# A hybrid decoder step: scaled tiles of the second norm tied to their splits, and four subtractions moved to GpSimd

## The chip, the cores and the metric

The kernel runs on one core of a Trainium2 chip. The metric is the device time of one execution in microseconds (us); the figure for a kernel is the median of its runs.

## What is computed

The reference is one decoder layer for 512 prompt tokens and 32 sample tokens (544 columns in all), with width 1024 and a feed-forward width of 2816. Only its end matters here:

```python
x = x + merged @ w_out
h2 = rmsnorm(x, norm2_g)
x = x + (silu(h2 @ w_ffn_gate) * (h2 @ w_ffn_up)) @ w_ffn_down
```

Ahead of it come the first norm, linear attention with a matrix state, dilated window attention, and the merge of both; behind it a last norm. Window caches of the sample tokens are also copied out.

## The kernel before

Activations lie transposed: 128 channels on the partitions, the 544 tokens along the free axis, cut into two halves of 272 columns (`cols`; index `i` or `hf_`, 0 or 1). A float32 number is carried as two parts, a high one that ScalarE makes by a copy into TensorE's rounded type and a low one, the difference, that VectorE makes (`split`, line 232: `act.activation` at L238, then `tt` at L230). Each product of matrices is three: high by high, low by high, high by low (`gemm`, line 327). Weights go through the same split (`wh`, `wlo`, two buffers each).

**The second norm.** For each half of the tokens the output projection is added to the residual `x2` (tiles `xres`), the squares are summed, `rates` makes the reciprocal root and `second` (line 1217) spreads it over the partitions by a small matmul into `zb`. Then eight scalar_tensor_tensor operations of VectorE (L1229, through the helper at L227) write the scaled tiles `hf{i}_{j}`, two for each of four tiles j, and four splits make `h2{i}h_{j}` and `h2{i}l_{j}`. For half 0 this happens within the projection of half 1. For half 1 `rates` and `second` are called in the middle of the matmuls of the first two feed-forward blocks on half 0 (`AT`, `mid`), so that TensorE has work while they run.

**The feed-forward.** Blocks 0 and 1 of gate (`fg`) and up (`fu`) run first on half 0 and then on half 1 (line 1252), block 0 into the wide PSUM tile `d`, of which there are two, block 1 into `zf`. Blocks 2 and 3 run plainly on both halves, each gemm into a `d`. `gated` takes them out: tanh on ScalarE (L1246), then two operations of VectorE on the tile `y`; a `d` is free when VectorE's operation has read it.

Blocks 4 to 21 go in pairs by a scheme of seven products (Strassen's, in Winograd's form) on 2 by 2 blocks: `mov` holds the seven operands made of tokens, `sta` those made of weights. Four of the token operands are sums of scaled tiles: `n5`, `n6`, `n4`, `n7`, each of two tiles of 128 x 544, made by `summed_up` (line 1288) on VectorE and split by `operand` (line 1276). Products 7 and 4 use `n7` and `n4`; the first of them comes some 26 us after the last low part. The weights' sums come by transfers: `fetch(0)` (line 1309) loads a block into `f0d` and `f0e` by SyncE's queue and adds a second block to them by two accumulating transfers that GpSimd issues (L1328, L1329). `prep_5` and `prep_7` then split `f0d` and `f0e` into `ws1` and `ws3`.

**What sets the order.** A planner orders each engine's instructions when the program is built, by its own estimates of when their inputs are ready; the engines then run their lists strictly in order. `pin` (`tc.keep_in_program_order`) ties an instruction behind the one that was written before it on its engine; it asks for order only, not for the end of that one. `nop` ties nothing. The two accumulating transfers in `fetch` are tied so, and so are the small copies `pace` on GpSimd (L298) and the transfers of window caches (L417) that follow a weight's split: `pace` reads a mark that the split's high part leaves, and thereby holds the next transfers of GpSimd's list back until that split is done.

```python
        nc.sync.dma_start(out=r2, in_=c2[:, 4:8])
        pin(pool.dma_start(out=s1, in_=c2[:, 4:8], accum_op=ALU.add))
        pin(pool.dma_start(out=s3, in_=c1[:, 0:4], accum_op=ALU.add))
```

In the program's text `fetch(0)` stands behind the last `operand` call, and on GpSimd nothing is written between the `pace` and cache copy of block 2's gate weights and these two transfers.

Of the kernel before, what the change touches and what calls it, by code (L numbers as in the profile page):

```python
# [5 lines left out]
F32 = mybir.dt.float32  # L6
# [3 lines left out]
AF = mybir.ActivationFunctionType  # L10
ALU = mybir.AluOpType
# [159 lines left out]
def build(tc, I, O, C):  # L171
    nc = tc.nc
    act, dve, pe, pool = nc.scalar, nc.vector, nc.tensor, nc.gpsimd
# [21 lines left out]
    def free(*tags):  # L195
        for t in tags:
            rings.pop(t)
# [18 lines left out]
    def dense_ps(ha=HA):  # L216
        t = psd.tile([P, 1024], F32, tag="d", name="d")
        return t[:, 512 - ha:512 - ha + NT]

    def mps(name="m", tag="m"):  # L220
        return psm.tile([P, 512], F32, tag=tag if SPLIT_PS else "m", name=name)

    def mm(out, lhsT, rhs, start=True, stop=True):
        return pe.matmul(out, lhsT=lhsT, rhs=rhs, start=start, stop=stop)  # L224

    def stt(out, in0, scalar, in1, op0, op1, **kw):
        return dve.scalar_tensor_tensor(out=out, in0=in0, scalar=scalar, in1=in1, op0=op0, op1=op1, **kw)  # L227

    def tt(out, a, b, op):
        return dve.tensor_tensor(out=out, in0=a, in1=b, op=op)  # L230

    def split(hi, lo, src, scale=1.0, pin=lambda i: i, later=None, **kw):
        def rest():
            if scale == 1.0:
                pin(tt(lo, src, hi.bitcast(F32), ALU.subtract))
            else:
                stt(lo, src, scale, hi.bitcast(F32), ALU.mult, ALU.subtract)
        pin(act.activation(out=hi, in_=src, func=AF.Copy, scale=scale, **kw))  # L238
        if later is None:
            rest()  # L240
        else:
            later.append(rest)

    def rsqrt(tp, x, n, tag, pin=lambda i: i):
        y = tp.tile([P, n], F32, name=tag + "i", tag=tag + "i")[:x.shape[0]]
        pin(pool.tensor_tensor(out=y, in0=x, in1=mhalf[0:x.shape[0], 0:n], op=ALU.pow))
        return y
# [54 lines left out]
    def dropped(keep):  # L302
        free(*[f"{keep}{n}{u}" for n in "hl" for u in range(2)])

    def weights(i, ahead=2, pin=lambda i: i, later=None):
        while state["next"] <= min(i + ahead, len(wl) - 1):
            emit_w(state["next"], pin, later)
            state["next"] += 1
        return ready[i]
# [12 lines left out]
    pin = tc.keep_in_program_order  # L322
# [4 lines left out]
    def gemm(i, xh, xl, halves=(0, 1), z=None, k0=0, first=True, last=True, ahead=2, cols=cols, fix=False, part=0, mid=None):  # L327
        _, _, nk, _, m, _ = wl[i]
        wide, m = m // P, min(m, P)
        wh, wlo = weights(i, ahead)  # L330
        if z is None:
            z = dense_ps()
        for k in range(nk):
            if mid and k == mid[0]:
                mid[1]()
            for j, (w, x) in enumerate(((wh, xh), (wh, xl), (wlo, xh))):
                for hf in halves:
                    (pin if fix else nop)(mm(z[hf] if type(z) is list else z[0:m, cols[hf][0]:cols[hf][1]], w(k * wide + part if wide > 1 else k), x(k0 + k, hf),
                       start=(first and k == 0 and j == 0), stop=(last and k == nk - 1 and j == 2)))
        due()  # L340
        return z
# [4 lines left out]
    def halved(ts):  # L346
        return lambda k, hf: ts[hf][k]
# [60 lines left out]
    for g in (2, 1, 0):  # L408
        step = (WIN[g] - 4) // (4 if g == 2 else 1)
        for nm in ("k", "v"):  # L410
            for b in range(8):
                for r0 in range(0, WIN[g] - 4, step):
                    src = I[f"state_win{g}_{nm}"][0, b, 4 + r0:4 + r0 + step].rearrange("r h d -> (r h d)").rearrange("(a n) -> a n", a=4)
# [14 lines left out]
    def late(t, ap, eng=None):  # L428
        tc.keep_in_program_order((eng or nc.gpsimd).dma_start(out=t, in_=ap))  # L429
        return t  # L430
# [4 lines left out]
    def vec_tile(name, ap, n):  # L435
        t = cst.tile([P, n], F32, name=name)
        nc.gpsimd.dma_start(out=t, in_=ap.rearrange("(k p) -> p k", p=P))
        return t

    def many(n, w, dt, name):  # L440
        return [one.tile([P, w], dt, name=f"{name}_{i}") for i in range(n)]
# [24 lines left out]
    for i in (0, 2, 1, 4, 3):  # L466
        n = x_src[i][1]
        j = junk[i % 2]
# [22 lines left out]
    zb = dense_ps(256)  # L491
# [677 lines left out]
    for m in range(8):  # L1169
        proj_a(m)  # L1170
        if m + AHEAD < 8:
            gate_a(m + AHEAD)
            if m + AHEAD == 7:
                free(*[f"{a}_{k}" for a in ("hh", "hl") for k in range(KD)])
                x2 = [late(t, xT_d[:, k]) for k, t in enumerate(many(KD, NT, F32, "xres"))]
# [3 lines left out]
    n2g = vec_tile("n2g", I["norm2_g"][0], 8)  # L1179
    h2h, h2l, hf = [], [], []  # L1180
    for i, (a_, b_) in enumerate(cols):
        n = b_ - a_
        acc = two.tile([P, HA], F32, tag="acc", name="acc")
        for m in range(8):
            z = [mps("zw")[:, 0:n]] * 2 if m % 2 else dense_ps()
            gemm(W["wo", m], halved(mgh), halved(mgl), halves=(i,), z=z, ahead=2 if i == 0 else W["fu", 0] - W["wo", m])
            z = z[i] if m % 2 else z[:, a_:b_]
            if i == 1:
                dropped(f"wo{m}")
                if m == FW:  # L1190
                    weights(W["fu", 1], 0, pin)
            tt(x2[m][:, a_:b_], x2[m][:, a_:b_], z, ALU.add)
            if m == 0:
                act.activation(out=acc[:, 0:n], in_=x2[m][:, a_:b_], func=AF.Square)
            else:
                sq = two.tile([P, HA], F32, tag="sq", name="sq")
                act.activation(out=sq[:, 0:n], in_=x2[m][:, a_:b_], func=AF.Square)
                tt(acc[:, 0:n], acc[:, 0:n], sq[:, 0:n], ALU.add)

        tiles = [(c, min(c + P, n)) for c in range(0, n, P)]  # L1200
        dgs = []

        def rates(i=i, acc=acc, tiles=tiles, dgs=dgs):
            zc = mps("zc")
            rt = two.tile([P, 3], F32, tag="rt", name="rt")
            dve.memset(rt, 1.0)
            for u, (c0, c1) in enumerate(tiles):
                (pin if i else nop)(mm(zc[0:c1 - c0, u:u + 1], acc[:, c0:c1], ones[:, 0:1]))
            for u, (c0, c1) in enumerate(tiles):
                dve.tensor_scalar(out=rt[0:c1 - c0, u:u + 1], in0=zc[0:c1 - c0, u:u + 1], scalar1=1.0 / D, scalar2=EPS, op0=ALU.mult, op1=ALU.add)  # L1210
            y = rsqrt(two, rt, 3, "r2")
            for u, (c0, c1) in enumerate(tiles):
                w_ = c1 - c0
                dgs.append(two.tile([P, P], F32, tag="dg2", name="dgt", bufs=3))
                dve.tensor_scalar(out=dgs[u][0:w_, 0:w_], in0=ident[0:w_, 0:w_], scalar1=y[0:w_, u:u + 1], scalar2=None, op0=ALU.mult)

        def second(i=i, a_=a_, b_=b_, n=n, tiles=tiles, dgs=dgs):
            zb = mps("zb")
            for (c0, c1), dgt in zip(tiles, dgs):
                w_ = c1 - c0  # L1220
                (pin if i else nop)(mm(zb[:, c0:c1], ones[0:w_, :], dgt[0:w_, 0:w_]))
            hi, lo = ([one.tile([P, 2, n], F32R, name=f"h2{i}{w}_{j}") for j in range(4)] for w in "hl")
            hf.append([one.tile([P, 2, n], F32, name=f"hf{i}_{j}") for j in range(4)])
            h2h.append([hi[k // 2][:, k % 2] for k in range(KD)])
            h2l.append([lo[k // 2][:, k % 2] for k in range(KD)])
            for j in range(4):
                for u in range(2):
                    m = 2 * j + u
                    stt(hf[i][j][:, u], x2[m][:, a_:b_], n2g[:, m:m + 1], zb[:, 0:n], ALU.mult, ALU.mult)  # L1229
                split(hi[j], lo[j], hf[i][j])  # L1230
            free(*[f"mg{i}_{m}" for m in range(8)])
            if i:
                free("acc", "sq", "rt", "r2i", "dg2")

        if i == 0:
            rates()
            second()
# [35 lines left out]
    def parts_of(h, l):  # L1273
        return [lambda k, t=t: t[k // 2][:, k % 2] for t in (h, l)]

    def operand(nm, src):
        hi, lo = ([one.tile([P, 2, HA], F32R, name=f"{nm}{w}_{j}") for j in range(2)] for w in "hl")
        for j in range(2):
            split(hi[j], lo[j], src[j])
        return parts_of(hi, lo)  # L1280

    def by_halves(i, k0):
# [5 lines left out]
    def summed_up(nm, f):  # L1288
        ts_ = [two.tile([P, 2, HA], F32, tag="nf", name=nm, bufs=4) for _ in range(2)]
        for j in range(2):  # L1290
            f(j, ts_[j])
        return ts_
# [5 lines left out]
    n4 = summed_up("n4", lambda j, t: stt(t, n6[j], -1.0, B21[j], ALU.mult, ALU.subtract))  # L1298
    mov[4] = operand("n4", n4)
    n7 = summed_up("n7", lambda j, t: tt(t, B22[j], B12[j], ALU.subtract))  # L1300
# [297 lines left out]
```

## Time and profile before

| what | us |
|---|---|
| median of 3 runs (lowest to highest) | 1061.74 (1059.97 to 1063.48) |
| the profiled execution, its own time | 1065.11 |
| its span in the trace | 1063.3 |
| TensorE (PE) busy | 1037.5 (98%) |
| VectorE (DVE) busy | 662.8 (62%) |
| ScalarE (ACT) busy | 458.6 (43%) |
| GpSimd (POOL) busy | 315.8 (30%) |

PE is TensorE's matmuls, PEld its weight loads. Times of rows count from the start of the span. A row of a timeline gives the start, the length, the engine, the line, the operation, the tile written and the tiles read, the shapes and the count, and in brackets how long the engine was idle before it and what it waited for. Neighbouring records overlap at their ends, since a next instruction enters the pipeline before the last has left it.

### The profile page before, as it was taken

To read this page: it belongs to the slowest core of one execution; us is meant where nothing else is said; L and a number is where in the kernel's file an instruction comes from. 1 tells how busy PE (TensorE), PEld (TensorE's weight loads), DVE (VectorE), ACT (ScalarE), POOL (GpSimd) and SP (SyncE) were. 2 spreads that over 40 slices of the span, in tenths; PEclk is the share of its full clock that TensorE was granted. 3 is DMA by queue.
4 is the path that set the end of the run, shared out by engine and by line. 5 is a ranking of instruction groups with operands and counts; after the bars stand their busy time and mean duration, and the time that the engine had idled before them with its cause. 6 is when DMAs were issued, how large, how long until landed. Compare 5 with 4: busy or idle time off the path is not lost.

```text
span 1063.3 us, 20293 instructions
## 1 busy us (share of the span) xinstructions
PE 1037.5 (98%) x7935; PEld 1001.0 (94%) x7935; DVE 662.8 (62%) x1232; ACT 458.6 (43%) x1016; POOL 315.8 (30%) x503
## 2 busy tenths in 40 slices
PE   6999999999999999999999999999999999999996
PEld 5999899899998999989989999999999999999996
DVE  5587665495686665636626566575988888933232
ACT  5454344663555543342323343353445454622222
POOL 2444232243453402222211211133343333122221
PEclk8999999999999999999999999999999999999998
DMA  8589537565586825536433554369999999443342
GB/s 236 139 223 259 164 96 203 152 201 171 162 267 193 284 65 171 177 114 199 145 98 119 164 159 129 100 186 225 281 261 275 274 298 250 153 151 102 113 114 84
DMA packets 207103, 190.30 MB, mean 179 GB/s; under 512 B 11120, under 2 KB 192080, under 8 KB 205728
## 3 DMA queue, kind: packets, MB, share of 16 engines
q0 software_dynamic: 35280, 95.63, 30.7%
q1 hardware_dynamic: 165440, 89.08, 30.2%
q10 hardware_dynamic: 6288, 4.29, 1.4%
q8 instruction: 62, 1.02, 0.4%
q14 instruction: 33, 0.27, 0.1%
HBM read 177.14 MB, written 55.67 MB: 219 GB/s over the span
## 4 chain that ended last, share of the span: by engine, by line
PE 90%; DMA 3%; DVE 3%; ACT 2%; issue 1%; POOL 0%; POOLq 0%; SPq 0%; DVEq 0%; ACTq 0%
PE d L224 61%; PE zs L224 9%; PE zo L224 5%; PE zB L224 3%; PE zw L224 2%; PE zl L224 2%; PE zA L224 1%; PE zu L224 1%; DMA raw<-in_w_out 1%; DMA f0e<-in_w_ffn_gate 1%; PE zq L224 1%; DMA x<-in_x_prompt 1%; PE zA L692 1%; DVE al L227 1%; PE zp L224 1%
## 5 line engine op out<-in xcount | busy, mean ns | idle before, releaser
L298 POOL COPY pace<-mark 1x1 f32<-1x1 f32 x109 | 82.1, 753 | 435.5 <-ACT wh L238 383.7
L224 PE MATMUL d<-hh,wh 128*128 128x272 f32 (+1 forms) x928 | 204.5, 298 | 4.2 <-ACT hh L238 2.2
L224 PE MATMUL d<-hl,wh 128*128 128x272 f32 (+1 forms) x928 | 202.6, 296 | 0.2 <-DVE hl L230 0.2
L238 ACT ACTIVATE wh<-raw 128x1024 fp32r<-128x1024 f32 (+1 forms) x97 | 100.3, 1034 | 232.4 <-PE d L224 152.7
L224 PE MATMUL d<-hh,wlo 128*128 128x272 f32 x912 | 196.6, 294 | 0.0
L230 DVE TENSOR_TENSOR wlo<-raw,wh 128x1024 fp32r<-128x1024 f32 (+1 forms) x96 | 115.4, 1202 | 101.1 <-ACT wh L238 100.8
L224 PEld LDWEIGHTS d<-hh,wh 128*128 128x128 f32 (+1 forms) x928 | 149.2, 190 | 7.7 <-ACT hh L238 2.3
L224 PEld LDWEIGHTS d<-hl,wh 128*128 128x128 f32 (+1 forms) x928 | 148.9, 190 | 4.0 <-issue 2.7
L224 PEld LDWEIGHTS d<-hh,wlo 128*128 128x128 f32 x912 | 146.1, 192 | 0.6
L224 PE MATMUL d<-al,wh 128*128 128x272 f32 x308 | 64.4, 291 | 2.0 <-DVE al L227 2.0
L224 PE MATMUL d<-ah,wh 128*128 128x272 f32 x308 | 64.9, 292 | 0.0
L224 PE MATMUL d<-ah,wlo 128*128 128x272 f32 x308 | 64.2, 290 | 0.0
L230 DVE TENSOR_TENSOR qb<-kt,qb 128x512 f32<-128x512 f32 x48 | 33.0, 688 | 44.7 <-DMA qb<-qd_d 44.4
L224 PEld LDWEIGHTS d<-al,wh 128*128 128x128 f32 x308 | 48.8, 190 | 2.5 <-DVE al L227 2.5
L224 PEld LDWEIGHTS d<-ah,wh 128*128 128x128 f32 x308 | 48.9, 191 | 0.1
L224 PEld LDWEIGHTS d<-ah,wlo 128*128 128x128 f32 x308 | 48.8, 190 | 0.0
L429 POOL DMA_DIRECT2D kt<-in_state_win_k x48 | 32.9, 685 | 12.2 <-DVE qb L230 7.5
L230 DVE TENSOR_TENSOR vl<-vt,vh 128x512 fp32r<-128x512 f32 (+1 forms) x40 | 25.0, 635 | 16.3 <-ACT vh L238 16.0
L238 ACT ACTIVATE vh<-vt 128x512 fp32r<-128x512 f32 (+1 forms) x40 | 23.0, 586 | 28.0 <-DMA vt<-in_state_win_v 17.3
L230 DVE TENSOR_TENSOR w12l<-raw,w12h 128x1024 fp32r<-128x1024 f32 x17 | 20.8, 1224 | 20.2 <-ACT w12h L238 20.2
L561 DVE TENSOR_REDUCE sall<-qb 128x8 f32<-128x512 f32 x48 | 32.7, 682 | 0.8
L429 POOL DMA_DIRECT2D vt<-in_state_win_v x40 | 21.7, 545 | 35.5 <-DVE vl L230 31.9
(562 smaller groups left out, 2831.8 us busy)
## 6 DMA issues: line engine op xcount, KB each, us to landing
raw<-in_w_in SPq DMA_DIRECT2D x58, 512.0 KB, 6.1
out_win_k_sample<-in_state_win_k POOLq DMA_DIRECT2D x32, 511.0 KB, 4.8
out_win_v_sample<-in_state_win_v POOLq DMA_DIRECT2D x32, 511.0 KB, 7.8
qb<-qd_d POOLq DMA_DIRECT2D x48, 256.0 KB, 5.1
kt<-in_state_win_k POOLq DMA_DIRECT2D x32, 256.0 KB, 5.3
vt<-in_state_win_v POOLq DMA_DIRECT2D x32, 256.0 KB, 4.3
raw<-in_w_ffn_down SPq DMA_DIRECT2D x16, 512.0 KB, 4.6
raw<-in_w_ffn_up SPq DMA_DIRECT2D x13, 512.0 KB, 6.3
```

The costliest lines, as they stand in the source:

```text
L224: return pe.matmul(out, lhsT=lhsT, rhs=rhs, start=start, stop=stop)
L227: return dve.scalar_tensor_tensor(out=out, in0=in0, scalar=scalar, in1=in1, op0=op0, op1=op1, **kw)
L230: return dve.tensor_tensor(out=out, in0=a, in1=b, op=op)
L238: pin(act.activation(out=hi, in_=src, func=AF.Copy, scale=scale, **kw))
L298: tc.keep_in_program_order(pool.tensor_copy(out=pace, in_=mark[0:1]))
L429: tc.keep_in_program_order((eng or nc.gpsimd).dma_start(out=t, in_=ap))
L561: dve.tensor_reduce(out=sall[:, g, 16 * b_:16 * b_ + 16].rearrange("p (t h) -> p t h", h=4)[:, :, 2 * hp:2 * hp + 2], in_=qb.rearrange("p ...
L692: pe.transpose(zA[:, v * P:(v + 1) * P], s[:, v * P:(v + 1) * P], ident)
```

## The change

In `second`, for half 1 alone, the scaled tiles and both parts of each split are tied in the order of the program's text, and that order is new: tiles 0, tiles 1, split 0, tiles 2, split 1, tiles 3, split 2, split 3. For half 0 the text's order is the same new one, but nothing is tied. In `operand` the splits are written out: the high part stays on ScalarE, the low part goes to GpSimd for `n4` and `n7` (two subtractions each) and stays on VectorE for `n5` and `n6`.

```diff
         def second(i=i, a_=a_, b_=b_, n=n, tiles=tiles, dgs=dgs):
             zb = mps("zb")
+            keep = pin if i else nop
             for (c0, c1), dgt in zip(tiles, dgs):
                 w_ = c1 - c0
                 (pin if i else nop)(mm(zb[:, c0:c1], ones[0:w_, :], dgt[0:w_, 0:w_]))
...
             for j in range(4):
                 for u in range(2):
                     m = 2 * j + u
-                    stt(hf[i][j][:, u], x2[m][:, a_:b_], n2g[:, m:m + 1], zb[:, 0:n], ALU.mult, ALU.mult)
-                split(hi[j], lo[j], hf[i][j])
+                    keep(stt(hf[i][j][:, u], x2[m][:, a_:b_], n2g[:, m:m + 1], zb[:, 0:n], ALU.mult, ALU.mult))
+                if j:
+                    split(hi[j - 1], lo[j - 1], hf[i][j - 1], pin=keep)
+            split(hi[3], lo[3], hf[i][3], pin=keep)
...
     def operand(nm, src):
         hi, lo = ([one.tile([P, 2, HA], F32R, name=f"{nm}{w}_{j}") for j in range(2)] for w in "hl")
         for j in range(2):
-            split(hi[j], lo[j], src[j])
+            act.activation(out=hi[j], in_=src[j], func=AF.Copy)
+            (pool if nm in ("n4", "n7") else dve).tensor_tensor(out=lo[j], in0=src[j], in1=hi[j].bitcast(F32), op=ALU.subtract)
         return parts_of(hi, lo)
```

## Rows read from the trace of the kernel before

**Rows 1.** Windows: PE, PEld, DVE, ACT, POOL busy us, clock, DMA share, GB/s.

```profile
680.00:700.00 20.00, 18.99 (x149) 18.62 (x149) 18.78 (x32) 11.34 (x20) 5.57 (x5) 1.00 0.16 54
700.00:720.00 20.00, 19.37 (x155) 19.19 (x154) 12.49 (x19) 7.19 (x14) 4.57 (x9) 1.00 0.80 232
720.00:740.00 20.00, 19.38 (x153) 19.01 (x152) 8.95 (x13) 6.38 (x13) 7.40 (x7) 1.00 0.97 215
740.00:800.00 60.00, 60.00 (x480) 60.00 (x479) 52.94 (x78) 29.90 (x53) 23.19 (x30) 1.00 1.08 264
```

**Rows 2.** Timeline of PE, the rows at its waits.

```profile
684.95 0.29 PE L224 MATMUL zf<-h21h,fu1h 128*128 128x272 f32 x1
686.25 0.39 PE L224 MATMUL d<-h21l,wh 128*128 128x272 f32 x1 [1.01 <-DVE h21l L230]
...
710.69 0.37 PE L224 MATMUL d<-h20h,wh 128*128 128x272 f32 x1 [0.63 <-DVE y L227]
...
739.02 0.40 PE L224 MATMUL d<-n6h,w24l 128*128 128x272 f32 x1 [0.62 <-DVE w24l L230]
```

**Rows 3.** Timeline of DVE.

```profile
681.58 3.35 DVE L227 SCALAR_TENSOR_TENSOR hf<-xres,n2g,zb 128x272 f32<-128x272 f32 x8
...
685.48 0.72 DVE L230 TENSOR_TENSOR h21l<-hf,h21h 128x544 fp32r<-128x544 f32 x1
...
695.86 0.72 DVE L230 TENSOR_TENSOR n<-hf,hf 128x544 f32<-128x544 f32 x1
...
701.75 0.72 DVE L230 TENSOR_TENSOR n7l<-n,n7h 128x544 fp32r<-128x544 f32 x1
...
707.64 0.69 DVE L230 TENSOR_TENSOR ws3l<-f0e,ws3h 128x512 fp32r<-128x512 f32 x1 [2.80 <-ACT ws3h L238]
...
709.83 0.71 DVE L227 SCALAR_TENSOR_TENSOR y<-y,d 128x544 f32<-128x544 f32 x1
```

**Rows 4.** Timeline of ACT.

```profile
682.51 0.66 ACT L238 ACTIVATE h21h<-hf 128x544 fp32r<-128x544 f32 x1 [1.32 <-DVE hf L227]
...
698.19 0.65 ACT L238 ACTIVATE n7h<-n 128x544 fp32r<-128x544 f32 x1
703.48 0.63 ACT L238 ACTIVATE ws1h<-f0d 128x512 fp32r<-128x512 f32 x1 [4.64 <-DMA f0d<-in_w_ffn_gate]
706.98 0.63 ACT L238 ACTIVATE ws3h<-f0e 128x512 fp32r<-128x512 f32 x1 [2.86 <-DMA f0e<-in_w_ffn_gate]
707.52 1.04 ACT L238 ACTIVATE wh<-raw 128x1024 fp32r<-128x1024 f32 x1
...
708.56 0.60 ACT L1246 ACTIVATE y<-d 128x544 f32<-128x544 f32 x1
```

**Rows 5.** Chain that ended last: start, length, what.

```profile
697.13 0.81 POOL f0d L1328
697.94 9.01 DMA f0e<-in_w_ffn_gate
...
710.69 12.23 PE d L224 x96
```

**Rows 6.** Timeline of POOL.

```profile
694.43 2.19 POOL L298 COPY pace<-mark 1x1 f32<-1x1 f32 x1 [18.22 <-ACT wh L238]
696.57 0.56 POOL L417 DMA_DIRECT2D out_win_v_sample<-in_state_win_v  x1
697.13 1.39 POOL L1328 DMA_DIRECT2D f0d<-in_w_ffn_gate  x1
697.94 1.90 POOL L1329 DMA_DIRECT2D f0e<-in_w_ffn_gate  x1
```

**Rows 7.** Groups of POOL instructions by shape, whole span: busy us, mean ns.

```profile
L933 POOL COPY qd<-q 128x512 f32<-128x512 f32 x4 | 2.5, 626 | 7.8 <-PE zs L224 7.8
```

**Rows 8.** Instructions that read the tile mark, ns min/median/max.

```profile
L298 POOL COPY pace<-mark x109: 173/892/2659, 16.6 to 1038.1; 1x1 f32<-1x1 f32 x109
```

**Rows 9.** Instructions that read the tile n7l, first and last start.

```profile
L224 PE MATMUL zs<-n7l,ws3h x72: 287/289/293, 728.9 to 910.6; 128*128 128x272 f32 x72
```

## The prediction

> **What bounds the kernel now.** I read the windows first. TensorE fills its stretches: around the change it is idle for 1.01 us in 680 to 700, 0.63 in 700 to 720 and 0.62 in 720 to 740, and not at all in the 60 us that follow, at a granted clock of 1.00 [rows 1]. So VectorE's work counts only where TensorE waits for it, and the three idle stretches, 2.26 us or 0.2% of the span, are all that this stage can give. The timeline of TensorE then shows one wait in each [rows 2]. At 685.24 it has done the four matmuls that want only the high part of the new half and stands until 686.25 for the first low part, `h21l`. At 710.06 it stands 0.63 us for VectorE to read a `d` that it wants for block 3. At 739.02 it waits for a weight's low part.
>
> The second wait is the one to look at, because the chain of waits runs through it. Behind `d` stands `y<-y,d` at 709.83 [rows 3], ahead of which ScalarE did, in this order, `ws1h`, `ws3h`, a weight's `wh` and the tanh of `y` [rows 4]. ScalarE stood until 706.98 for `f0e` to land, and only then came to the tanh, although the product that the tanh reads had long been there: 96 matmuls of this kind take 12.23 us [rows 5], so a gemm of 48 takes 6.1, and with TensorE running dry at 710.06 block 2's gate product ended near 704.0. The chain goes back through 9.01 us of the transfer into `f0e` to GpSimd, which issued `f0d` and `f0e` at 697.13 and 697.94 [rows 5, 6]. The end of the kernel thus hangs, at this place, on when GpSimd issues two transfers.
>
> **The tied order.** Nothing is removed: eight scaled tiles, four high parts, four low parts as before. VectorE runs the eight scaled tiles in 3.35 us, 0.41 apart, from 681.58, and the first low part starts at 685.48 after another operation that the planner put between [rows 3]; its high part was ready at 682.51 + 0.66 = 683.17 [rows 4]. Tied, the first low part comes fifth: 681.58 + 4 x 0.41 = 683.22, done at 683.94. TensorE wants it at 685.24, so the wait of 1.01 us goes, with 1.3 us to spare; one operation of 0.72 put between is covered too. Late next are the other high parts, since scaled tiles now wait behind low parts, each 0.64 from start to start (0.72 with the overlap): tiles 2 come 0.64 later than before, tiles 3 1.28, so the last high part ends near 686.9 and its low part near 687.6. TensorE needs 24 matmuls, about 3.0 us, for each tile j if it goes through all four products with it, and then has cover to spare; if the planner lets it run one product through all tiles, it wants tiles 3 some 2.25 us after 684.6, at 686.85, and stands up to 0.8 us. Gain 0.2 to 1.01; I take 1.01, because work of three other products lies ready.
>
> **The four subtractions.** Four operations of 0.72 us leave VectorE [rows 3]. It was busy 18.78 of 20 us there [rows 1], but no TensorE wait hangs on its load behind 686, so this is worth nothing by itself. On GpSimd nobody needs their results soon: the first matmul that reads `n7l` starts at 728.9 [rows 9], which hides them by far.
>
> What counts is GpSimd's list. The two accumulating transfers are tied behind what is written before them on GpSimd, which was a cache transfer and is now the last `n7l`. That one needs the last `n7h`, which ScalarE ends at 698.19 + 0.65 = 698.84 [rows 4], already past 697.13. The trace has no subtraction of this size on GpSimd. From below: a copy of 128 x 512 takes 626 ns [rows 7], for 544 columns 0.67 us. From above: a GpSimd copy of one element took 2.19 us at 694.43, against a shortest of 0.17 and a median of 0.89 [rows 8]; it ended within 0.05 us of a VectorE operation with two SBUF inputs, the one at 695.86 [rows 3, 6], as if held off by VectorE. I take twice the copy, 1.33 us, for two inputs read one after the other. [...]
>
> Starting when the cache transfer is issued, four subtractions last from 697.13 to 697.13 + 4 x 1.33 = 702.45, so `f0d` and `f0e` are issued 5.3 us later; with 0.67 they last to 699.8 (2.7 later), with 2.19 to 705.9 (8.8 later). What precedes may come up to 1.0 earlier with TensorE, so 4.3 net, between 1.7 and 8.8. Queued behind the transfers on GpSimd are `pace` copies and cache transfers, for which nobody in this stage waits; SyncE's loads go by their own queue.
>
> **Where that goes** depends on the planner's order on ScalarE. (a) If `ws1h` and `ws3h` stay ahead of `wh` and the tanh, the chain moves one for one with `f0e`, and the 1.01 gained above is eaten, since TensorE only arrives earlier at the same wait. (b) If the planner sees `f0e` land after 704.0, it puts `wh` and the tanh first. With both `ws` behind them the second wait vanishes too: -1.01 - 0.63 = -1.64. With only `ws3h` behind: `f0d` lands at 702.45 - 1.0 + (703.48 - 697.13) = 707.8, and by the spacing of the rows (0.54 to the next, 1.04, 1.27, 0.86 to TensorE) TensorE goes on at 711.5 instead of 710.69: +0.8. The planner had `f0e` landing before 704 by its own reckoning, else the order would not be what it is; a delay of several microseconds probably takes it past that.
>
> **Forecast**: (b), the middle of -1.64 and +0.8, -0.4 us. Against the profiled execution's 1065.11 that is 1064.7; the median of the runs lies 3.4 below the profiled one, so 1061.74 - 0.4 = 1061.3. Chance 0.5; alone its range is 1060.1 to 1062.6.
>
> **Rivals.**
> Order kept, (a): TensorE waits for `f0e` at block 3. +4.3, so 1066.0 (1.7 to 8.8: 1063.4 to 1070.5). For it: in the order of before both splits stood ahead, and ScalarE already stood for them. Against it: `f0e` took 9.01 us and `f0d` 6.35 with other loads beside them, and a later issue may find the queues emptier, which gives back up to 2.7. It decides, against my forecast, once `n7l` ends over 1 us after 697.13, and it passes the bound of 0.3% (3.2 us, about what a measurement of this kernel can tell from no change) where the net delay is over 3.2. Chance 0.35, two thirds of it beyond that bound.
>
> The tie does nothing: the wait at 686.25 becomes one of 0.8 for the later tiles, or the gain is waited away at 710, with `f0e` as late as before. Then 1061.5 to 1061.9. For it speaks that TensorE's order is planned anew. Chance 0.1.
>
> VectorE held by GpSimd: subtractions that keep VectorE out for their whole length take 4 x 1.33 = 5.3 us from it (8.8 at the upper bound), and 2.9 have been taken off its list. It ended its work on this stage at 701.75 + 0.72 = 702.47 [rows 3] and the `d` for block 2's second product is wanted near 704.0, so it has 1.5 us in hand; it costs from there, at most 8.8 - 2.9 - 1.5 = +4.4, 1066.1, and nothing at 1.33 (5.3 - 2.9 - 1.5 = 0.9). [...] Chance 0.05, of which half slower.
>
> **How the numbers follow.** Slower by over 0.3%: two thirds of 0.35 and half of 0.05, 0.26. Faster by over 0.3% would take 3.2 us where the idle of the stage is 2.26, so it needs an order changed elsewhere or a lucky median: 0.08. The rest is 0.66. The range goes from (b)'s lower end of 1060.1, less 0.3 for the spread of a median whose runs lay 1.75 apart to either side, 1059.8, to 1066.4, a little past the value of the kept order, leaving out its upper third.
>
> **What would show it.** Right: the first `h21l` starts near 683.2 and TensorE's gap of 1.01 us is gone; `f0d` is issued 2 to 6 us later behind four GpSimd subtractions of 0.7 to 2.2 us; on ScalarE `wh` and the tanh stand ahead of `ws3h`; TensorE's wait before block 3 is under 2 us. Wrong: `ws3h` still ahead of the tanh and a wait of 4 us or more at block 3; or the two transfers planned early after all, with the subtractions already done; or a low part that now waits for its high part and holds the scaled tiles behind it.

## The result, and the profile after

| kernel | median us (lowest to highest) | runs |
|---|---|---|
| before | 1062.17 (1059.97 to 1066.27) | 6 |
| changed | 1068.15 (1066.07 to 1071.02) | 6 |

The ratio is 1.0053, with a 95% interval of 1.0036 to 1.0070: 5.6 us slower (3.8 to 7.4). The forecast was 1061.3 and its range ended at 1066.4. The profiled execution took 1069.32 us, its span 1067.5.

The windows of the changed kernel answer to [rows 1]; the short one comes from narrower windows of the same view.

```profile
680.00:700.00 20.00, 17.38 (x137) 17.02 (x136) 17.56 (x28) 11.54 (x20) 6.36 (x3) 1.00 0.05 13
700.00:720.00 20.00, 17.50 (x126) 17.35 (x127) 12.73 (x16) 5.26 (x12) 10.58 (x15) 0.91 0.67 171
720.00:740.00 20.00, 20.00 (x162) 20.00 (x161) 6.50 (x10) 4.68 (x9) 7.41 (x7) 1.00 1.02 246
740.00:800.00 60.00, 59.57 (x474) 59.35 (x473) 53.07 (x78) 30.10 (x53) 22.21 (x26) 1.00 1.08 276
...
703.00:705.00 2.00, 2.00 (x11) 2.00 (x10) 2.00 (x3) 0.00 (x0) 2.00 (x4) 0.50 0.05 20
```

TensorE was idle for 2.26 us in these 120 us before [rows 1]; now it is idle for 5.55, and a stretch behind 702 also runs at a granted clock of 0.50 (703 to 705 above). TensorE's timeline says at which matmuls it stood (answers to [rows 2]).

```profile
700.86 0.37 PE L224 MATMUL d<-h20h,wh 128*128 128x272 f32 x1 [3.48 <-DVE y L227]
...
703.30 0.43 PE L224 MATMUL d<-h21l,wh 128*128 128x272 f32 x1
703.52 0.43 PE L224 MATMUL d<-h20h,wlo 128*128 128x272 f32 x1
...
716.28 0.37 PE L224 MATMUL d<-h20h,wh 128*128 128x272 f32 x1 [1.64 <-DVE y L227]
```

The wait of 1.01 us for `h21l` is gone, as forecast. In its place TensorE stands 3.48 us before block 2, for VectorE to read the `d` of block 0's gate product, and 1.64 us before block 3, where it stood 0.63. The matmuls from 702.20 to 705.56 start 0.226 us apart where they otherwise start 0.125 apart: 15 x 0.10 = 1.5 us more. The sum is -1.01 - 0.63 - 0.19 (from 0.62 to 0.43 at the weight's low part, at 739 before and near 744 now) + 3.48 + 1.64 + 1.5 = +4.8, within the measured interval.

Two traces do not start alike: the matmuls into `zb` of half 0, ahead of all that is tied, start at 654.16 before and at 654.76 in the changed kernel, so 0.6 us of every later difference between the two traces lies ahead of the stage (over all traces of this study that start lies between 650.1 and 654.8). From there to `zb` of half 1 both take 26.43 us, so the new order of half 0 costs nothing; from there to the first matmul that reads `n7l` (728.9 before, 734.5 now) the changed kernel takes 5.0 us longer, near the 4.8.

The chain shows what led to the 3.48. Two rows of before's chain first, not shown so far, then the changed kernel's.

```profile
691.18 1.90 PE d L224 x15
...
693.14 0.70 ACT wh L238
```

```profile
688.86 1.51 PE d L224 x12
690.37 1.50 PE zf L224 x12
...
695.47 0.57 ACT wh L238
...
698.26 1.82 DVE w22l L230
```

In the changed kernel TensorE goes through blocks 0 and 1 tile by tile, twelve matmuls into `d` and twelve into `zf` in turn. Before, it ran the last 15 matmuls that the chain follows into `d` in one piece and left `zf` for the end. So block 0's gate product is there 2.3 us later (695.47 against 693.14 at the `wh` that ScalarE does behind it; 1.7 without the shift of 0.6), and TensorE has used up the work that lay ready. Why the tiles come so late is seen on VectorE (answers to [rows 3]), the last low part of the kernel before first:

```profile
689.01 0.72 DVE L230 TENSOR_TENSOR h21l<-hf,h21h 128x544 fp32r<-128x544 f32 x1
```

```profile
684.44 0.72 DVE L230 TENSOR_TENSOR h21l<-hf,h21h 128x544 fp32r<-128x544 f32 x1
...
689.61 0.71 DVE L230 TENSOR_TENSOR h21l<-hf,h21h 128x544 fp32r<-128x544 f32 x1
690.24 0.71 DVE L1283 TENSOR_TENSOR n5l<-n,n5h 128x544 fp32r<-128x544 f32 x1
...
691.51 0.71 DVE L230 TENSOR_TENSOR h21l<-hf,h21h 128x544 fp32r<-128x544 f32 x1
...
696.65 1.69 DVE L230 TENSOR_TENSOR wlo<-raw,wh 128x1024 fp32r<-128x1024 f32 x1 [0.62 <-ACT wh L238]
698.26 1.82 DVE L230 TENSOR_TENSOR w22l<-f0c,w22h 128x512 fp32r<-128x512 f32 x1
700.01 0.71 DVE L227 SCALAR_TENSOR_TENSOR y<-y,d 128x544 f32<-128x544 f32 x1
```

Among the tied instructions the planner put token sums and their low parts, so the last `h21l` ends at 692.2, 10.1 us behind the first scaled tile at 682.17; before, it ended at 689.7, 8.2 us behind the one at 681.58. TensorE never stands for it here, since its order reads it first at 694.72. Ahead of the read of `d` stand `wlo` and `w22l`, which take 1.69 and 1.82 us; in the kernel before the same two took 1.22 and 0.68. GpSimd's list (answers to [rows 6]) has the subtractions where the forecast had them:

```profile
693.64 5.90 POOL L1283 TENSOR_TENSOR n4l<-n,n4h 128x544 fp32r<-128x544 f32 x2 [16.82 <-ACT n4h L1282]
...
700.68 2.66 POOL L1283 TENSOR_TENSOR n7l<-n,n7h 128x544 fp32r<-128x544 f32 x2
703.28 1.38 POOL L1332 DMA_DIRECT2D f0d<-in_w_ffn_gate  x1
704.12 1.86 POOL L1333 DMA_DIRECT2D f0e<-in_w_ffn_gate  x1
```

Both transfers are issued 6.2 us later than in [rows 6] (5.6 without the shift), and ScalarE keeps the order of [rows 4]: it waits for `f0d` and `f0e`, and only then does `wh` and the tanh that free block 3's `d`.

```profile
710.29 0.63 ACT L238 ACTIVATE ws1h<-f0d 128x512 fp32r<-128x512 f32 x1 [10.74 <-DMA f0d<-in_w_ffn_gate]
712.57 0.63 ACT L238 ACTIVATE ws3h<-f0e 128x512 fp32r<-128x512 f32 x1 [1.65 <-DMA f0e<-in_w_ffn_gate]
713.11 1.05 ACT L238 ACTIVATE wh<-raw 128x1024 fp32r<-128x1024 f32 x1
...
714.15 0.60 ACT L1249 ACTIVATE y<-d 128x544 f32<-128x544 f32 x1
```

### The profile page after: what moved, and what is told of

Read it like the earlier page. It is cut to its first block, busy times and chain, and to the rows that moved or that the text cites. A ratio compares the mean times of both kernels' runs of the same rounds, so it can differ in the third digit from the quotient of the medians.

```text
span 1067.5 us, 20294 instructions
## 1 busy us (share of the span) xinstructions
PE 1037.8 (97%) x7935; PEld 1001.2 (94%) x7935; DVE 664.2 (62%) x1228; ACT 459.0 (43%) x1016; POOL 325.9 (31%) x507
## 5 line engine op out<-in xcount | busy, mean ns | idle before, releaser
L230 DVE TENSOR_TENSOR wlo<-raw,wh 128x1024 fp32r<-128x1024 f32 (+1 forms) x96 | 118.5, 1235 | 103.3 <-ACT wh L238 102.8
```

## The experiments

All but the last two in one table, each against runs of the kernel before that were taken with it (medians 1061.41 to 1063.88); the times in us are the ratio and its interval times 1062. Idle is TensorE's in 680 to 800 of the profiled execution, the clock the granted one in 680 to 700 and in 700 to 720.

| kernel | ratio to before | us to before | idle us | clock |
|---|---|---|---|---|
| before | | | 2.26 | 1.00, 1.00 |
| changed | 1.0053 | +5.6 (3.8 to 7.4) | 5.55 | 1.00, 0.91 |
| the tie alone | 1.0011 | +1.2 (-0.4 to 2.7) | 2.79 | 0.91, 1.00 |
| the subtractions alone | 1.0001 | +0.1 (-1.3 to 1.6) | 1.80 | 1.00, 1.00 |
| changed, transfers early | 1.0062 | +6.6 (4.7 to 8.5) | 8.23 | 0.88, 0.86 |
| before, transfers early | 0.9995 | -0.5 (-1.8 to 0.7) | 1.03 | 1.00, 1.00 |
| the tie, sums late | 1.0030 | +3.2 (1.3 to 5.0) | 3.85 | 1.00, 0.91 |
| changed, subtractions behind the transfers | 1.0021 | +2.2 (0.6 to 3.8) | 2.47 | 0.93, 0.98 |
| the tie, sums late, transfers early | 0.9988 | -1.3 (-2.9 to 0.3) | 1.13 | 1.00, 1.00 |
| changed, `w22` late | 1.0012 | +1.3 (-0.2 to 2.8) | 3.76 | 1.00, 1.00 |
| changed, whole products | 1.0036 | +3.8 (2.1 to 5.5) | 4.63 | 0.83, 1.00 |
| sums late, transfers early, with the subtractions | 1.0007 | +0.7 (-0.8 to 2.3) | 1.85 | 1.00, 1.00 |

**The two halves apart.** The first kernel has only the part of the diff in `second`, the second only the part in `operand`.

> Only the tie; all eight low parts stay on VectorE. Theory A (the tie itself costs: with the low parts early, TensorE's list takes the four products of blocks 0 and 1 side by side, so block 0's gate product ends some 2.3 us later and its d is read too late for block 2): the 1.01 us wait is gone, a wait of 2 to 3 us stands before block 2, one of 0.5 to 1.5 before block 3; 1 to 3 us slower than before. Theory B (all of the loss comes from GpSimd: its subtractions hold VectorE and the two transfers): no wait before block 2, 1.0 us faster than before.

> Only the four subtractions on GpSimd; the second norm as before. Theory A: the 1.01 us wait stays, no wait before block 2, since block 0's gate product ends early as before; f0d is issued 4 to 7 us later; before block 3 a wait of 1 to 3 us; 0.5 to 2 us slower than before. Theory B: 4 to 6 us slower than before, most of it before block 3 or through VectorE operations stretched to 1.5 to 4 us.

With the tie alone the 1.01 us go and a wait before block 2 comes; the one before block 3 is gone.

```profile
696.18 0.47 PE L224 MATMUL d<-h20h,wh 128*128 128x272 f32 x1 [2.45 <-DVE y L227]
...
698.48 0.43 PE L224 MATMUL d<-h20h,wlo 128*128 128x272 f32 x1
698.71 0.43 PE L224 MATMUL d<-h21h,wlo 128*128 128x272 f32 x1
```

Behind the wait TensorE again runs 15 matmuls at 0.23 us from start to start, +1.5. The tie gives back all that it gained and perhaps a little more. The subtractions alone come out at nothing. Three engines of that kernel, GpSimd, VectorE, ScalarE:

```profile
694.14 2.69 POOL L1280 TENSOR_TENSOR n4l<-n,n4h 128x544 fp32r<-128x544 f32 x2
696.79 2.66 POOL L1280 TENSOR_TENSOR n7l<-n,n7h 128x544 fp32r<-128x544 f32 x2
699.40 1.35 POOL L1329 DMA_DIRECT2D f0d<-in_w_ffn_gate  x1
```

```profile
694.11 6.42 DVE L230 TENSOR_TENSOR wlo<-raw,wh 128x1024 fp32r<-128x1024 f32 x1
```

```profile
700.96 1.06 ACT L238 ACTIVATE wh<-raw 128x1024 fp32r<-128x1024 f32 x1 [5.15 <-PE d L224]
...
704.82 0.63 ACT L238 ACTIVATE ws1h<-f0d 128x512 fp32r<-128x512 f32 x1 [2.71 <-DMA f0d<-in_w_ffn_gate]
705.36 0.61 ACT L1246 ACTIVATE y<-d 128x544 f32<-128x544 f32 x1
```

A subtraction takes 1.34 us here. One `wlo` took 6.42 us beside all four: 1.22 and 5.2, about what they last. And ScalarE has `wh` ahead of `ws1h` and the tanh ahead of `ws3h`: this is case (b) of the forecast, and block 3 does not wait. Together the halves cost 5.6, apart 1.2 and 0.1: some 4 us are theirs only in company. Of the expectations theory A came nearer, but its wait before block 3 came in neither kernel, nor its loss from the subtractions.

**The transfers' place.** `fetch(0)` is written ahead of half 1 of blocks 0 and 1, in the changed kernel and in the one before.

```diff
     for hf_ in range(2):
+        if hf_ == 1:
+            fetch(0)
         for m in range(2):
...
-    fetch(0)
     for m in range(2, PLAIN):
```

> The changed kernel with the block fetch(0) moved ahead of the feed-forward on half 1, so that the two accumulating transfers are issued before the subtractions. Theory A with stretched VectorE operations: the wait before block 3 (1.6 us) is gone, the wait before block 2 stays at 3 to 5 us with a lower granted clock behind it; 2.5 to 5 us slower than the kernel before. Theory B in its form with the transfers alone: both waits go, 1 us faster than the kernel before to no change.

> The kernel before with the same early fetch(0). Both theories: the transfers land some 15 us earlier, the wait of 0.63 us before block 3 is gone and the 1.01 us wait stays; 0.6 us faster than before, at most 0.3 us slower if the two weight splits that now stand earlier on ScalarE and VectorE hold a tanh or a read of d.

In the kernel before, the waits before block 3 and at 739 go and the 1.01 stays; the time is the same within its interval. In the changed one the wait before block 3 goes too, but the one before block 2 is far longer than the 3 to 5 us expected: the splits of `f0d` and `f0e` now stand ahead of the read of `d`, with a `wlo` that takes 4.38 us beside subtractions.

```profile
700.55 0.57 PE L224 MATMUL d<-h20h,wh 128*128 128x272 f32 x1 [7.85 <-DVE y L227]
```

So late transfers are not the whole cost, and what counts before block 2 is how much of VectorE's list comes ahead of that read, and at what length.

**The subtractions' place.** The changed kernel, the four subtractions written behind `fetch(0)` and tied.

```diff
+            if nm in ("n4", "n7"):
+                late_lo.append((lo[j], src[j], hi[j]))
...
     fetch(0)
+    for lo_, s_, h_ in late_lo:
+        pin(pool.tensor_tensor(out=lo_, in0=s_, in1=h_.bitcast(F32), op=ALU.subtract))
```

> The changed kernel with the four GpSimd subtractions written and tied behind the two accumulating transfers instead of ahead of them. Theory A (GpSimd and VectorE hold each other off, and the transfers stand behind the subtractions): f0d is issued near 696 instead of 703, the two VectorE splits ahead of the read of d take 1.2 and 0.7 us again, so the wait before block 2 falls from 3.5 to 1 to 2.5 us and the one before block 3 to under 0.7; some VectorE operation with two inputs from the on-chip memory near 700 takes 3 to 7 us instead; within 2 us of the kernel before. Rival D (the subtractions cost by their length on GpSimd wherever they stand): still 4 us or more slower than before.

```profile
697.01 0.37 PE L224 MATMUL d<-h20h,wh 128*128 128x272 f32 x1 [1.88 <-DVE y L227]
```

`f0d` is issued at 696.18 again, no wait comes before block 3, `wlo` and `w22l` take 1.23 and 0.68 us, and the wait before block 2 is 1.88. The operation of 3 to 7 us that was expected on VectorE did not come; the longest there is a `wlo` of 1.82 behind the read of `d`. Of the 5.6 us 3.4 are gone; the 2.2 that are left agree with the tie's 1.2 within the intervals.

**What stands ahead of the read.** The changed kernel, the split into `w22` tied behind those of `f0d` and `f0e`.

```diff
-        sta[x, 4] = form("w22", raws[x][2])
+        sta[x, 4] = form("w22", raws[x][2], **({} if x else {"pin": pin}))
```

> The changed kernel, with the split of f0c into w22 tied behind the splits of f0d and f0e, so that w22l no longer stands between wlo and the read of d. Theory, the wait before block 2 is the sum of what VectorE's list puts ahead of that read: 3.48 falls by the 1.82 us that w22l took, to 1.4 to 2.0, and the planner's new order on ScalarE (wh and the tanh ahead of ws3h) takes away the 1.64 before block 3; 2.5 to 4.5 us less than the changed kernel, ratio to before 1.001 to 1.003. Rival, the read of d waits for TensorE's product and the tanh alone: the wait stays at 3 to 3.6 and the ratio at 1.004 or more.

```profile
695.91 0.37 PE L224 MATMUL d<-h20h,wh 128*128 128x272 f32 x1 [1.74 <-DVE y L227]
...
709.13 0.37 PE L224 MATMUL d<-h20h,wh 128*128 128x272 f32 x1 [0.99 <-DVE y L227]
```

The wait falls from 3.48 to 1.74, by as much as `w22l` is out of the way (1.82), though TensorE's order was planned anew too. Behind this wait the granted clock stays at 1.00 (695 to 699), and the 1.5 us are saved as well in this execution. ScalarE now has `wh` and the tanh between `ws1h` and `ws3h`, and the wait before block 3 falls from 1.64 to 0.99.

**The late tiles.** Two kernels. In the first, the tie alone with the sums `n5`, on which `n6` and `n4` rest, tied behind what is written before them, which puts all sums behind block 1's last `y`. In the second, the changed kernel with the matmuls of blocks 0 and 1 tied product after product on half 1 too.

```diff
-    n5 = summed_up("n5", lambda j, t: tt(t, B11[j], B12[j], ALU.subtract))
+    n5 = summed_up("n5", lambda j, t: pin(tt(t, B11[j], B12[j], ALU.subtract)))
```

```diff
-                     fix=hf_ == 0, mid=(AT[m, nm], rates if m == 0 else second) if hf_ == 0 and (m, nm) in AT else None)
+                     fix=True, mid=(AT[m, nm], rates if m == 0 else second) if hf_ == 0 and (m, nm) in AT else None)
```

> The tie alone, and the first token sum (n5, and with it all that follows from it) tied behind the last operation on block 1's y, so that VectorE's list holds only splits and y between the scaled tiles and block 2. Theory A (the tie costs because TensorE's products then run side by side, and on VectorE the read of d stands behind token sums and splits): no wait before block 2 or one below 0.5 us, the 1.01 us wait gone; 1 us faster than before, if the wait before block 3 stays near 0.6. Rival C (side by side, block 0's product simply ends too late, whatever stands on VectorE): the wait before block 2 stays at 2 us or more, 1 us slower than before.

> The changed kernel, with the matmuls of blocks 0 and 1 on half 1 tied product after product, where the planner had them side by side, tile by tile. Theory, the late tiles are the cause and the order only chooses where TensorE stands: by VectorE's rows the low parts of tiles 2 and 3 end at 690.3 and 692.2, TensorE with 0.75 us of work for each tile of one product stands 3.5 to 4.5 us in 685 to 692, the gate product ends near 693, and before block 2 it stands under 0.5; ratio 1.004 to 1.007, as the changed kernel. Rival, the side by side order is itself the fault: the tiles come in time, the wait before block 2 goes and no other takes its place; ratio 1.002 or less.

Without sums between the tied instructions the last low parts end at 687.6, and TensorE does not wait at all in 680 to 700. Its order has changed back in part: the last 22 matmuls into `d` run in one piece again, and the `wh` behind block 0's gate product comes 10.4 us after the first scaled tile, against 11.6 before and 13.3 in the changed kernel.

```profile
686.27 1.35 DVE L230 TENSOR_TENSOR h21l<-hf,h21h 128x544 fp32r<-128x544 f32 x2
```

The sums now stand ahead of `wlo` and the read of `d` for block 3 instead, and the wait there is 3.41 us:

```profile
711.98 0.57 PE L224 MATMUL d<-h20h,wh 128*128 128x272 f32 x1 [3.41 <-DVE y L227]
```

So the wait before block 2 went as theory A has it, but the kernel is slower than before and not 1 us faster. With whole products TensorE waits for the tiles themselves, 4.0 us in all, and not before block 2:

```profile
682.74 0.39 PE L224 MATMUL d<-h21l,wh 128*128 128x272 f32 x1 [1.07 <-DVE h21l L230]
...
685.81 0.39 PE L224 MATMUL d<-h21l,wh 128*128 128x272 f32 x1 [2.05 <-DVE h21l L230]
...
687.71 0.60 PE L224 MATMUL d<-h21l,wh 128*128 128x272 f32 x1 [0.89 <-DVE h21l L230]
```

Behind these waits TensorE ran at a granted clock of 0.50 until 693.8, some 2.7 us more. So neither order is free of the late tiles: it chooses where they are paid for. An order between the two was not tried. The ratio was under the expected 1.004, though the interval reaches past it.

**The remedy for both.** The tie, sums late and transfers early; then the same with the subtractions on GpSimd.

> The tie alone, the late token sums, and the early fetch(0) of the kernel with early transfers. If theory A holds: the waits before blocks 2 and 3 are both gone, and the 1.01 us wait too; 1.6 us faster than before, the sum of the two. Rival C: a wait of 2 us or more before block 2 stays, 1 us slower than before.

> The best version so far (the tie, the token sums tied late, the two transfers written early; ratio 0.9988) with the four subtractions on GpSimd. They now stand behind the two transfers in GpSimd's list, near 705 to 712, and TensorE's order is that of the best version. Theory, GpSimd's subtractions hold VectorE wherever a product waits for its read of d: operations of VectorE with two SBUF inputs stretch by 2.7 to 5.3 us in 704 to 713, and TensorE stands 1 to 4 us before a product of block 3; ratio 1.000 to 1.003. Rival, the harm lay only in the transfers queued behind the subtractions: no new wait in 700 to 720 and a ratio within 0.0007 of 0.9988.

The first has no wait in 680 to 720, and 0.54 and 0.59 us for weights' low parts behind that. It has the lowest ratio of this study, though its interval reaches past 1. With the subtractions neither expectation came out whole: VectorE is held as the one said (two sums take 3.06 us and two weights' low parts 1.85 each, two of these rows below), but no read of `d` comes too late; two waits of 0.82 and 1.03 us at weights' parts near 735 take the place of the 1.13. The trace is of this kernel's fastest run (1061.32 against a median of 1064.72), so it does not show what the median paid.

```profile
705.38 3.06 DVE L230 TENSOR_TENSOR n<-hf,hf 128x544 f32<-128x544 f32 x2
...
710.13 1.85 DVE L230 TENSOR_TENSOR w12l<-f0a,w12h 128x512 fp32r<-128x512 f32 x1
```

The two ratios lie 0.0019 apart and their intervals overlap, so whether the subtractions cost anything there stays open; nothing shows that they gain.

**What holds VectorE.** The kernel before with other work on GpSimd in place of the four subtractions, one run each: copies, which read one tile, and constants, which read none. The subtraction is left out of both.

```diff
-            split(hi[j], lo[j], src[j])
+            act.activation(out=hi[j], in_=src[j], func=AF.Copy)
+            if nm in ("n4", "n7"):
+                pin(pool.tensor_copy(out=lo[j], in_=src[j]))
+            else:
+                tt(lo[j], src[j], hi[j].bitcast(F32), ALU.subtract)
```

```diff
-                pin(pool.tensor_copy(out=lo[j], in_=src[j]))
+                pin(pool.memset(lo[j].bitcast(F32), 0.0))
```

> The kernel before with the four low parts of n4 and n7 replaced by plain GpSimd copies of one 128 x 544 input (the subtraction is left out). If GpSimd operations that read with one input hold VectorE off as those with two do: each copy takes about 0.7 us, and the VectorE split beside them takes 1.2 us plus the 2.7 us of the four, near 3.9 us. If only two inputs conflict: that split stays at 1.2 us.

> The kernel before, with the four low parts of n4 and n7 written by GpSimd as constants (the subtraction is left out), so that GpSimd reads no SBUF tile there. Theory, what keeps VectorE out is GpSimd's reading: the block's low part wlo beside the four operations takes its usual 1.22 us, against 6.42 beside four subtractions and 2.90 beside four copies. Rival, any long operation of GpSimd keeps a VectorE operation with two SBUF inputs out: wlo takes 1.9 us or more. The 1.01 us wait near 686 stays under both.

The `wlo` beside the copies; then the first two constants, and the `wlo` that ran beside them:

```profile
696.78 2.90 DVE L230 TENSOR_TENSOR wlo<-raw,wh 128x1024 fp32r<-128x1024 f32 x1
```

```profile
695.76 1.06 POOL L1281 MEMSET n4l<- 128x544 f32 x2
```

```profile
695.75 1.23 DVE L230 TENSOR_TENSOR wlo<-raw,wh 128x1024 fp32r<-128x1024 f32 x1
```

Copies stretch `wlo` from 1.22 to 2.90 us, between the two expectations: it was done at 699.68, before the last copy was at 700.17. Constants leave it at 1.23. So in these runs `wlo` was held beside operations of GpSimd that read a tile (6.42 us beside subtractions, 2.90 beside copies) and not beside ones that read none (1.23). Their times, 1063.92 and 1067.86, are of one run each and prove nothing.

## Why the prediction was wrong

**The first step that failed** is in "The tied order": "the last high part ends near 686.9 and its low part near 687.6". The low part ended at 692.2, or 691.6 without the shift of 0.6 between the traces. Tied instructions keep their order, but others may be put between, and the planner put seven there (sums, their low parts, a `y`), some 4.2 us in all. The prediction had the first of these before its eyes (it allowed for "one operation of 0.72 put between") and took the rest for absent. With the sums kept out the step holds: 687.6 from a first scaled tile at 681.39, and no wait.

**From it follows the second**: "Gain 0.2 to 1.01; I take 1.01, because work of three other products lies ready". The gain came, but the three other products were spent on bridging the late tiles. That the planner chose this order because of the tiles is in no trace; the kernel with the sums late, where the tiles are early and the order goes back in part, speaks for it. Block 0's gate product was finished 1.7 us later (2.3 with the shift), and before VectorE had read it TensorE had nothing left. Tying whole products shows the late tiles as 4.0 us of waits for the tiles themselves.

**The third** is "no TensorE wait hangs on its load behind 686, so this is worth nothing by itself". That was read off the kernel before, whose read of `d` was done 0.7 us ahead of the need:

```profile
696.50 0.71 DVE L227 SCALAR_TENSOR_TENSOR y<-y,d 128x544 f32<-128x544 f32 x1
```

```profile
697.90 0.29 PE L224 MATMUL d<-h20h,wh 128*128 128x272 f32 x1
```

Once the product behind it came later, VectorE's list decided: `w22l` out of it takes 1.74 us off the wait.

**Order kept or changed.** The forecast took (b), "a delay of several microseconds probably takes it past that". With the subtractions alone (b) is what came. In the changed kernel the order of (a) stayed, and TensorE waited 1.64 at block 3: of the sign of being wrong that the prediction names, `ws3h` ahead of the tanh came, the wait of 4 us or more did not. The planner's estimates are in no trace, so why it kept that order is not shown; that taking `w22` away brought (b) in part shows how near the two lie. The price of (a) was reckoned as 4.3 at block 3; there it was 1.0 more than before, because TensorE came 4.6 us later itself (714.64 against 710.06; 4.0 without the shift). One delay hid the other.

**VectorE held by GpSimd** got 0.05. No row of the kernel before shows a subtraction that keeps VectorE out; the runs show VectorE held: with the subtractions alone one `wlo` took 6.42 us, 1.22 + 5.2, about what the four last (694.14 to 699.45), and beside constants 1.23. At the place where the rival was priced the price was near as well: in the first of these two kernels 0.63 us of wait came at block 2's second product, against 0.9 by the prediction's own sum at 1.33 us for each, which it called nothing. It was not asked what it does when the tie has used up the slack: `wlo` and `w22l` took 0.47 and 1.14 us longer, 1.6 of the 3.48. Moving the subtractions behind the transfers brings both to their usual length and the wait to 1.88.

**The clock** has no term in the prediction; in the profiled execution it cost 1.5 us.

**What was right**: the 1.01 us went; a subtraction took 1.34 us where 1.33 was taken, though no run shows that it is because two inputs are read one after the other; `f0d` was issued 5.6 us later (6.2 with the shift) where 5.3 was taken, 4.3 net of an earlier TensorE that did not come.

So three things make the 5.6 us: late tiles, which go when the sums are kept out of the tied stretch (the sums then need a place of their own, or block 3 pays 3.41 us); GpSimd's subtractions beside VectorE's parts of weights; and transfers queued behind them. The two last go together when the subtractions are moved, so how they share those 3.4 us is known only from the waits.

## What to carry to other kernels

A tie fixes an order, not a density: look for what the scheduler may put between tied instructions, or tie that away too. When a wait is removed by spending work that lay ready, ask what that work was covering next, and follow the read that frees the next buffer. Two edits that each cost little or nothing alone may share the same slack; run them apart before they are judged together.

## What the runs showed of the hardware

In several runs GpSimd's operations that read a tile and VectorE's operations with two SBUF inputs took longer side by side. One `wlo`, 1.22 us in the kernel before, took 6.42 beside four subtractions in a row and 2.90 beside four copies; beside constants it took 1.23. In the kernel with whole products one subtraction, 1.34 us in the kernel with the subtractions alone, took 4.76, from 689.06 to 693.82, while VectorE ran such operations back to back until 692.60. In the case of 6.42 and in that of 4.76 the longer one ended only behind the whole row of the others: `wlo` at 700.53 behind subtractions that ended at 699.45, the subtraction at 693.82 behind 692.60. Elsewhere it did not: in the changed kernel a `wlo` was done at 698.34, while the two `n4l` took from 693.64 to 699.54. What decides who comes next is not shown. VectorE's reads of `d` into `y`, with one of the two inputs in PSUM, took 0.70 to 0.72 us, also beside subtractions (0.71 at 695.05 in the kernel with `w22` late, whose `n4l` took from 690.43 to 696.34).

TensorE's granted clock fell in or just behind its waits of 1.88, 2.45, 3.41, 3.48 and 7.85 us. It was at 0.50 from 712 to 714 behind the 3.41, from 703 to 705 behind the 3.48 and from 700 to 704 around the end of the 7.85; behind the 1.88 and the 2.45 the windows of 2 us show means of 0.56 to 0.58, with matmuls 0.23 us apart as behind the 3.48. It was back at 1.00 some 3 to 5 us after TensorE went on; behind the 2.45 and the 3.48 this cost 1.5 us each. With whole products, where waits of 1.07, 2.05 and 0.89 us lie between 681.7 and 687.7, the windows from 688 to 692 show 0.50, and matmuls start 0.23 us apart until 693.8. At the waits of 1.01, 1.64 and 1.74 us it stayed at 1.00 (684 to 690 before, 712 to 720 in the changed kernel, 695 to 699 with `w22` late). Near 920, behind the stage of the change, the kernel before and the changed one have the same wait of 2.00 us: before, the clock fell behind it to 0.50 (922 to 924); in the changed kernel it stayed at 1.00 (922 to 932). So in these traces the length of a wait alone does not decide it. The kernel before first, then the changed one:

```profile
920.06 0.52 PE L224 MATMUL d<-al,wh 128*128 128x272 f32 x2 [2.00 <-DVE al L227]
```

```profile
925.30 0.52 PE L224 MATMUL d<-al,wh 128*128 128x272 f32 x2 [2.00 <-DVE al L227]
```

So what a trace shows of the clock's cost behind a wait of about 2 us is one execution's, and so are the sums that hold it.
